# Dividing the mixer's input-projection tiles once and loading their parts from DRAM afterwards

## The chip, the cores and the metric

The kernel runs on one core of one Trainium2 chip. The metric is the device time of one execution in microseconds (us): the median of three runs before the change is 2557.08 us (2554.28 to 2558.01). About 0.2% (5 us) is what a measurement of this kernel can tell from no change.

## The reference

One decoder layer serves a prompt (2048 rows behind 16 prepended meta rows) and a sample group (8 sequences of 4 rows) with the same weights. All arithmetic is float32. Cut to what matters here:

```python
h = rmsnorm(x, norm_mix)
proj = h @ w_in                                  # 1024 -> 2560 + 8
lru_x, lru_gate, z, xbc, dt_raw = split(proj)    # 512, 512, 512, 1024, 8
xc  = causal_dwconv(lru_x, 4 taps);  hl = rg_lru(xc)          # a linear scan along the rows
lru_out = rmsnorm(hl * gelu(lru_gate), lru_out_norm)
xbc_c = silu(causal_dwconv(xbc, 4 taps));  ys = ssd_chunked(...)   # chunks of 128 rows, a state between them
ssd_out = rmsnorm(ys * silu(z), ssd_out_norm)
x = x + concatenate([lru_out, ssd_out]) @ w_out  # 1024 -> 1024
h = rmsnorm(x, norm_ffn)
u = causal_dwconv(h @ w_up, 3 taps);  x = x + (gelu(u[:, :3072]) * u[:, 3072:]) @ w_down
y = rmsnorm(x, norm_final)
```

The final states of the convolutions, of the LRU and of the SSD are outputs too.

## The kernel before, in words

**Divided operands.** TensorE multiplies in a rounded float32 format (F32R). To keep float32 accuracy each operand is divided into a high part (a rounded copy) and a low part (what the copy left): `divide` (L108) is one copy on ScalarE (`whi`, L109) and one subtraction on VectorE (`wlo`, L110). A product is then three matmuls, high by high, high by low, low by high. A weight tile is 128 x 1024 float32, 512 KB. The class `Plain` (L112) holds one: `load` brings it into a place with the tag `wraw` (two places), and `split` divides it into a pair of places with the tags `whi` and `wlo` (three pairs).

**Phase A, the mixer.** The rows are cut into six super-tiles (`PLAN_A`, L28): the sample and meta rows with two blocks of the prompt (N = 304 columns), then four of three blocks (N = 384), then one of two blocks (N = 256). For each super-tile all of `w_in` (20 weight tiles) and all of `w_out` (8 weight tiles) are loaded and divided again. The order of the main steps in one super-tile is: the small projection for dt; eight `xbc_main` steps; four `lru_main`; four `gate_main`; four `z_main`; then the output projection, `out_main` (L813): for each half of the output columns and each part of the inputs a pair of `w_out` tiles, and for each block of rows one step of 12 matmuls with 512 columns. A projection step (`project`, `group_mm`) takes one `w_in` tile and is 24 matmuls with N columns. The convolutions, gates, scans and chunks are side tasks, hung behind main steps by the table `SLOTS` (L41) and woven in by `weave` (L273).

**Phase B, the feed-forward part**, runs over four super-tiles of 512 rows; it has classes of its own for weights that it divides once and keeps in DRAM. The change does not touch them.

**What sets the order.** TensorE's order is as written. The order of the other engines, and that of the DMA issues on SyncE's queue (all DMAs of the kernel are issued there), is planned when the program is built, from estimated costs; a place with a tag is given on when all readers of the tile in it are done. The loop at the end of `build` (L297 to L316) walks the program: before each step it issues loads for weight tiles that are at most `AHEAD` = 2 past those the step uses, and divisions in the same way (none ahead until the first super-tile has begun, at `START2`).

**Rows of x.** `out_main` loads a 128 x 512 piece of x (`xo`, three places, L822), adds the product to it on VectorE (L826), and stores it to DRAM (`x2d`, L832) from SyncE's queue as soon as the second part is added. `Normed` (L161) normalises and transposes the rows of the next super-tile into `hhi` and `hlo`, both 128 x 8 x 546, in the pool `hh`, which stays open through phase A.

Of the kernel before, what the change touches and what calls it, by code (L numbers as in the profile page):

```python
# [8 lines left out]
F32 = mybir.dt.float32  # L9
F32R = mybir.dt.float32r  # L10
# [7 lines left out]
P = 128  # L18
D = 1024
NS, NSS, NM = 8, 4, 16  # L20
SROWS = NS * NSS
# [13 lines left out]
START = len(PLAN_A[0])  # L35
START2 = 3 * START + 1
GT_BUFS = 2
LOADS_B1, LOADS_B, SPLITS_B = 4, 3, 3


SLOTS = {  # L41
# [18 lines left out]
    "last": {  # L60
# [5 lines left out]
    },  # L66
# [7 lines left out]
def build(tc, i, o):  # L74
# [5 lines left out]
    with contextlib.ExitStack() as es:  # L80
# [5 lines left out]
        dp = es.enter_context(tc.tile_pool(name="scr", bufs=1, space=DRAM))  # L86
        xr = es.enter_context(tc.tile_pool(name="xr", bufs=1, side="right"))
        side = es.enter_context(contextlib.ExitStack())
        hh = side.enter_context(tc.tile_pool(name="hh", bufs=1, side="right"))
        phase = es.enter_context(contextlib.ExitStack())  # L90
        ja = phase.enter_context(tc.tile_pool(name="ja", bufs=1))
        junks = [lambda: ja.tile([P, D], BF16, name="junk", tag="junk")]
# [19 lines left out]
        class Plain:  # L112


            def __init__(self, src, room=lambda: wp.tile([P, 1024], F32, name="wraw", tag="wraw", bufs=2)):
                self.src, self.room = src, room
# [5 lines left out]
            def split(self, E=V):  # L122
                hi, lo = (wp.tile([P, 1024], F32R, name=nm, tag=nm) for nm in ("whi", "wlo"))
                divide(hi, lo, self.raw, E)
                self.out = hi, lo, self.raw

        def mms(ps, pairs):
            for k, (l, r) in enumerate(pairs):
# [32 lines left out]
        class Normed:  # L161


            def __init__(self, tiles):
                self.tiles = tiles
                self.h = None
                self.x = {}

            def alloc(self):
                if self.h is None:  # L170
                    self.h = [hh.tile([P, 8, NFMAX], F32R, name=nm, tag=nm) for nm in ("hhi", "hlo")]

            def load(self, q):
                src, off, rows = self.tiles[q]
# [109 lines left out]
                setattr(k, nm, v)  # L284

        k.tail = lambda: None
        h_b = Normed(b_tiles(k))
        phase_a(k, h_b)
        phase_b(k, h_b)

# [6 lines left out]
        for n, (fn, srcs) in enumerate(prog):  # L297
            if n < START:
                fn()
                continue  # L300
            if n == START2:
                begin.close()
            bound = len(flat) if n > k.begin_b else early
            b = n > k.begin_c
            while loaded < min(bound, used + len(srcs) + (LOADS_B if b else LOADS_B1 if n > k.begin_b else AHEAD)):
                flat[loaded].load()
                loaded += 1
            while split < min(bound, used + len(srcs) + (SPLITS_B if b else AHEAD if n >= START2 else 0)):
                flat[split].split(*(() if split else (G,)))
                split += 1  # L310
            ws = [z.out for z in flat[used:used + len(srcs)]]
            used += len(srcs)
            if fn is k.tail:
                end = es.enter_context(tc.manual_schedule(engines=order))
                continue
            fn(*ws)  # L316


def b_tiles(k):
    tiles, off = [], 0  # L320
    for t in PLAN_B[0]:
        rows = SROWS + 2 if t == "m" else P
        tiles.append((lambda t=t: (k.x2m if t == "m" else k.x2d[t], True), off, rows))
        off += rows
    return tiles
# [136 lines left out]
def phase_a_tile(k, E, c, si, columns, norm, norm2, x_src):  # L462
# [240 lines left out]
    def lru_main(j):  # L703
        def fn(w):
            T_.xc[j] = conv(j, project(w), c["lcw"][:, j, :], c["lcb"][:, j:j + 1], c["st_lc"][:, j], c["o_lc"][:, j])
        return fn
# [106 lines left out]
    def out_main(half, part, q):  # L813
        hcol = slice(half * 512, half * 512 + 512)

        def fn(*w):
            t, off, T = cols[q]
            if w:
                T_.w2 = w
            if part == 0:  # L820
                x = T_.xo[q] = tmp("xo", 512, bufs=3)
                ld(x[:T], x_src(t)[:, hcol])  # L822
            ps = psum("mm")
            k.tile_mm(ps, T_.w2, T_.y[0], T_.y[1], range(4 * part, 4 * part + 4), off, T)
            x = T_.xo[q]
            V.scalar_tensor_tensor(x[:T], ps[:T, :], T_.rs[part, q][:T], x[:T], op0=MUL, op1=ADD)  # L826
            if part == 1:
                if t == "m":
                    ld(k.x2m[0:SROWS, hcol], x[0:SROWS, :])
                    ld(k.x2m[SROWS:SROWS + 2, hcol], x[MISC - 2:MISC, :])  # L830
                else:
                    ld(k.x2d[t][:, hcol], x)  # L832
        return fn

    for j in range(8):
        main.append((xbc_main(j), (i["w_in"][12 + j],)))
    main.insert(int(first), (dt_main, ()))
    for j in range(4):
        main.append((lru_main(j), (i["w_in"][j],)))
    for j in range(4):  # L840
        main.append((gate_main(j), (i["w_in"][4 + j],)))
    for j in range(4):
        main.append((z_main(j), (i["w_in"][8 + j],)))
    for half in range(2):
        for part in range(2):
            for q in range(nt):
# [15 lines left out]
            tasks[f"misc{z}"] = lambda z=z: misc_blocks(3 * z, 3 * z + 3)  # L862

    if last:
        tasks["gain"] = lambda: ld(k.gain, i["gffn"])
    for q in range(nn):
        tasks[f"norm{q}"] = lambda q=q: norm2.norm(q)
# [525 lines left out]
```

## Time and profile before

| | us |
|---|---|
| median of three runs | 2557.08 |
| the profiled execution's own time | 2560.49 |
| its span, first to last instruction | 2558.4 |
| first super-tile of phase A, from 23 us | 160 |
| second to fifth super-tile, each | 158 to 160 |
| sixth super-tile | 121 |
| phase B, from 942 us | 1616 |

In the profile an engine's name stands for its work: PE matmul on TensorE, PEld its weight loads, DVE VectorE, ACT ScalarE, POOL GpSimd, SPq the queue of DMA issues on SyncE. A row of groups reads: line, engine, operation, out<-in by the program's names, shapes, count, then busy time, mean ns of one, idle time of the engine just before them, and what ended that idle time. A row of waits reads: who waited for whom, us in total, how often, the longest. A row of windows reads: stretch, length, busy us of each engine with its count of instructions, the granted TensorE clock, the busy share of the DMA engines, GB/s. Matmuls overlap: the duration of one is longer than the distance to the next.

### The profile page before, as it was taken

What the parts mean: (1) busy time and instruction counts of PE and PEld (TensorE: products, weight loads), DVE (VectorE), ACT (ScalarE), POOL (GpSimd) and SP (SyncE); (2) the same over time, 40 slices, a digit from 0 to 9 for tenths busy, and PEclk for the clock granted to TensorE, in tenths of its full rate; (3) what the DMA queues carried; (4) which work ended last, traced back from release to release, by engine and by line L of the source; (5) the groups of instructions that cost most, each with busy time, mean ns of one, the idle gap of its engine ahead of it and who ended that gap; (6) DMA issues with size and microseconds to landing.
All of it is one profiled execution on the core that took longest, in us unless ns stands there. A gap on an engine that the chain in (4) does not pass through costs nothing.

```text
span 2558.4 us, 42298 instructions
## 1 busy us (share of the span) xinstructions
PE 2450.5 (96%) x15834; PEld 2228.0 (87%) x15834; DVE 1953.8 (76%) x3028; ACT 1215.5 (48%) x2005; POOL 737.9 (29%) x1059
## 2 busy tenths in 40 slices
PE   7999998999999898999998999999999999999998
PEld 6788887888888888988886999998999998999997
DVE  7879878788787877776767877777877777877776
ACT  5545546455464655454455433434433434433333
POOL 5524333243242435545454201102101102100001
PEclk9999999999999999999999999999999999999999
DMA  5353252532525377554556866665866665866663
GB/s 183 119 180 98 90 173 70 183 98 87 171 75 173 110 229 257 185 198 178 197 201 236 300 249 226 221 218 214 313 227 214 214 220 189 316 214 214 218 223 123
DMA packets 153800, 486.39 MB, mean 190 GB/s; under 512 B 23334, under 2 KB 23718, under 8 KB 153596
## 3 DMA queue, kind: packets, MB, share of 16 engines
q1 hardware_dynamic: 153596, 483.70, 54.8%
q8 instruction: 125, 2.05, 0.3%
q14 instruction: 79, 0.65, 0.1%
HBM read 413.27 MB, written 70.37 MB: 189 GB/s over the span
## 4 chain that ended last, share of the span: by engine, by line
PE 60%; DVE 13%; issue 10%; POOL 7%; ACT 6%; DMA 4%; SPq 0%; POOLq 0%; DVEq 0%; ACTq 0%
PE mm L129 23%; PE sg L1116 14%; PE tr L129 9%; PE yy L129 9%; DVE cv L496 3%; DVE wlo L110 3%; ACT whi L109 2%; POOL wraw L958 2%; POOL wraw L957 1%; ACT ws L109 1%; POOL o_fc L1101 1%; POOL x L959 1%; DVE xi L741 1%; DMA wraw<-in_w_out 1%; DMA wk<-ws 1%
## 5 line engine op out<-in xcount | busy, mean ns | idle before, releaser
L110 DVE TENSOR_TENSOR wlo<-wraw,whi 128x1024 fp32r<-128x1024 f32 x358 | 456.0, 1275 | 147.3 <-ACT whi L109 146.3
L109 ACT ACTIVATE whi<-wraw 128x1024 fp32r<-128x1024 f32 x359 | 379.0, 1057 | 317.6 <-PE mm L129 141.8
L129 PE MATMUL mm<-hhi,whi 128*128 128x384 f32 (+4 forms) x1344 | 434.9, 324 | 13.9 <-ACT xr L491 10.5
L1116 PE MATMUL sg<-whi,ph 128*128 128x512 f32 x1320 | 425.1, 395 | 6.2 <-DVE acc L1120 6.2
L129 PE MATMUL mm<-hlo,whi 128*128 128x384 f32 (+4 forms) x1344 | 425.7, 317 | 0.9 <-DVE hlo L202 0.9
L129 PE MATMUL mm<-hhi,wlo 128*128 128x384 f32 (+4 forms) x1344 | 424.9, 316 | 0.0
L1101 POOL COPY o_fc<-u 128x2 f32<-128x2 f32 x192 | 85.9, 447 | 807.0 <-DVE u L1010 683.4
L1105 DVE SCALAR_TENSOR_TENSOR c<-u,fcw,c 128x512 f32<-128x512 f32 (+1 forms) x384 | 298.4, 791 | 23.0 <-ACT c L1103 13.4
L1116 PEld LDWEIGHTS sg<-whi,ph 128*128 128x128 f32 x1320 | 248.8, 189 | 65.5 <-DVE acc L1120 8.0
L129 PEld LDWEIGHTS mm<-hhi,whi 128*128 128x128 f32 x1344 | 258.3, 192 | 20.6 <-ACT xr L491 12.6
L129 PEld LDWEIGHTS mm<-hlo,whi 128*128 128x128 f32 x1344 | 257.8, 192 | 3.3 <-DVE hlo L202 1.2
L1116 PE MATMUL sg<-wlo,ph 128*128 128x512 f32 x660 | 259.7, 394 | 0.9 <-DVE wlo L110 0.9
L129 PEld LDWEIGHTS mm<-hhi,wlo 128*128 128x128 f32 x1344 | 257.9, 192 | 0.0
L1103 ACT ACTIVATE c<-u,fcb,fcw 128x512 f32<-128x512 f32 (+1 forms) x192 | 157.8, 823 | 111.8 <-DVE u L1010 109.2
L129 PE MATMUL yy<-h,ws 128*128 128x256 f32 x1476 | 195.5, 282 | 0.0
L129 PE MATMUL tr<-h,ws 128*128 128x256 f32 x1440 | 190.8, 282 | 1.2 <-DMA ws<-wk 1.2
L129 PE MATMUL mm<-h,ws 128*128 128x256 f32 x1404 | 185.9, 282 | 0.0
L129 PEld LDWEIGHTS yy<-h,ws 128*128 128x128 f32 x1476 | 184.8, 189 | 1.0
L129 PEld LDWEIGHTS tr<-h,ws 128*128 128x128 f32 x1440 | 180.1, 189 | 2.0 <-issue 1.3
L129 PEld LDWEIGHTS mm<-h,ws 128*128 128x128 f32 x1404 | 175.5, 189 | 0.5
L496 DVE SCALAR_TENSOR_TENSOR cv<-xr,packed,cv 128x384 f32<-128x384 f32 (+2 forms) x216 | 146.1, 677 | 6.9 <-ACT cv L494 4.2
L1120 DVE TENSOR_TENSOR acc<-acc,sg 128x512 f32<-128x512 f32 x165 | 112.7, 683 | 45.6 <-PE sg L1116 44.5
(311 smaller groups left out, 4983.7 us busy)
## 6 DMA issues: line engine op xcount, KB each, us to landing
ws<-wk SPq DMA_DIRECT2D x288, 512.0 KB, 5.0
wraw<-in_w_in SPq DMA_DIRECT2D x120, 512.0 KB, 3.6
wraw<-in_w_up SPq DMA_DIRECT2D x97, 512.0 KB, 4.7
wk<-ws SPq DMA_DIRECT2D x96, 512.0 KB, 6.6
wraw<-in_w_down SPq DMA_DIRECT2D x94, 512.0 KB, 4.9
wraw<-in_w_out SPq DMA_DIRECT2D x48, 512.0 KB, 3.6
wraw<-in_w_up SPq DMA_DIRECT2D x72, 256.0 KB, 5.5
x<-in_w_up SPq DMA_DIRECT2D x23, 512.0 KB, 6.8
```

Of the source, the lines that this page charges most:

```text
L109: A.activation(hi, raw, AF.Copy)
L110: E.tensor_tensor(lo, raw, hi.bitcast(F32), op=SUB)
L129: PE.matmul(ps, l, r, start=(k == 0), stop=(k == len(pairs) - 1))
L496: V.scalar_tensor_tensor(cv[:, 3:W], buf[:, t:t + NC], w[:, t:t + 1], cv[:, 3:W], op0=MUL, op1=ADD)
L741: V.tensor_tensor_scan(h[:, 3:W], a4[:, j, 3:W], m4[:, j, 3:W], hc[:, j:j + 1], op0=MUL, op1=ADD)
L957: G.tensor_tensor(v1, v0, v1, op=ADD)
L958: G.tensor_tensor(v0, g0, v0, op=SUB)
L1101: G.tensor_copy(o_fc[:, g, NS, :], u[:, W - 2:W])
L1103: A.activation(cv[:, 2:W], u[:, 2:W], AF.Identity, scale=fcw[:, g, 2:3], bias=c["fcb"][:, g:g + 1])
L1105: V.scalar_tensor_tensor(cv[:, 2:W], u[:, z:z + W - 2], fcw[:, g, z:z + 1], cv[:, 2:W], op0=MUL, op1=ADD)
L1116: PE.matmul(ps, l, r, start=first and n == 0, stop=last and n == len(seq) - 1)
L1120: V.tensor_tensor(xv, xv, ps, op=ADD)
```

## The change

In the first super-tile a `w_in` tile is loaded and divided as before, and both parts are also stored to DRAM, from ScalarE's queue: those of one tile are issued when the next one is divided. In the five later super-tiles a `w_in` tile is not divided: both parts are loaded from DRAM (two transfers of 512 KB in place of one), up to four tiles ahead. They go in turn into five places: three times the pair `whi` and `wlo`, then a new pair `xhi` and `xlo`, then the two `wraw` places. `w_out` tiles are loaded and divided as before, two ahead, through `wraw`. Loads of kept parts are not written before all divisions ahead of them are.

For room, `hhi` and `hlo` are 384 columns wide in phase A, in a pool `pa` beside the new pair, and in the last super-tile a new task `swap`, behind the last projection, closes that pool and opens `hh` with 546 columns for phase B's rows. The stores of `x2d` move from SyncE's queue to ScalarE's, each behind the addition of the next step.

```diff
-LOADS_B1, LOADS_B, SPLITS_B = 4, 3, 3
+LOADS_B1, LOADS_B, SPLITS_B, KEPT_AHEAD = 4, 3, 3, 4
...
-        15: "chunk41 norm0 lru1", 16: "norm1 lru2", 17: "norm2 lru3", 19: "ssd0 ssd1", 20: "rstd0 ssd2",
+        15: "chunk41 norm0 lru1", 16: "norm1 lru2", 17: "norm2 lru3", 19: "ssd0 ssd1", 20: "rstd0 ssd2 swap",
...
-        hh = side.enter_context(tc.tile_pool(name="hh", bufs=1, side="right"))
+        pa = side.enter_context(tc.tile_pool(name="pa", bufs=1, side="right"))
...
+        kept, late = {}, []
+
+        class Kept:
+
+            rooms = itertools.cycle("wwwxr")
+
+            def __init__(self, key, src):
+                self.key, self.plain = key, Plain(src)
+                self.ahead = KEPT_AHEAD
+
+            def load(self):
+                if self.key not in kept:
+                    kept[self.key] = [dp.tile([P, 1024], F32, name=f"{nm}_{self.key}", tag=f"{nm}_{self.key}")
+                                      for nm in ("khi", "klo")]
+                    self.plain.load()
+                    return
+                room = next(self.rooms)
+                if room == "w":
+                    parts = [wp.tile([P, 1024], F32R, name=nm, tag=nm) for nm in ("whi", "wlo")]
+                elif room == "x":
+                    parts = [pa.tile([P, 1024], F32R, name=nm, tag=nm) for nm in ("xhi", "xlo")]
+                else:
+                    parts = [wp.tile([P, 1024], F32, name="wraw", tag="wraw", bufs=2).bitcast(F32R) for z in range(2)]
+                for part, src in zip(parts, kept[self.key]):
+                    ld(part.bitcast(F32), src)
+                self.out = (*parts, None)
+
+            def split(self, E=V):
+                self.plain.split(E)
+                self.out = self.plain.out
+                store()
+                late.extend((z, part.bitcast(F32)) for z, part in zip(kept[self.key], self.out))
+
+        def store():
+
+            for dst, src in late:
+                A.dma_start(dst, src)
+            late.clear()
...
-                    self.h = [hh.tile([P, 8, NFMAX], F32R, name=nm, tag=nm) for nm in ("hhi", "hlo")]
+                    pool, n = (k.hh, NFMAX) if self.last else (pa, NMAX)
+                    self.h = [pool.tile([P, 8, n], F32R, name=nm, tag=nm) for nm in ("hhi", "hlo")]
...
-            while loaded < min(bound, used + len(srcs) + (LOADS_B if b else LOADS_B1 if n > k.begin_b else AHEAD)):
+            while loaded < bound:
+                ahead = LOADS_B if b else LOADS_B1 if n > k.begin_b else getattr(flat[loaded], "ahead", AHEAD)
+                if loaded >= used + len(srcs) + (ahead if n >= START2 else AHEAD):
+                    break
+                if getattr(flat[loaded], "key", None) in kept:
+
+                    if split < loaded:
+                        break
+                    split += 1
                 flat[loaded].load()
                 loaded += 1
-            while split < min(bound, used + len(srcs) + (SPLITS_B if b else AHEAD if n >= START2 else 0)):
+            while split < min(loaded, used + len(srcs) + (SPLITS_B if b else AHEAD if n >= START2 else 0)):
...
             V.scalar_tensor_tensor(x[:T], ps[:T, :], T_.rs[part, q][:T], x[:T], op0=MUL, op1=ADD)
+            k.store()
             if part == 1:
                 if t == "m":
-                    ld(k.x2m[0:SROWS, hcol], x[0:SROWS, :])
-                    ld(k.x2m[SROWS:SROWS + 2, hcol], x[MISC - 2:MISC, :])
+                    k.late.append((k.x2m[0:SROWS, hcol], x[0:SROWS, :]))
+                    k.late.append((k.x2m[SROWS:SROWS + 2, hcol], x[MISC - 2:MISC, :]))
                 else:
-                    ld(k.x2d[t][:, hcol], x)
+                    k.late.append((k.x2d[t][:, hcol], x))
+            if half == 1 and part == 1 and q == nt - 1:
+                k.store()
...
-        main.append((xbc_main(j), (i["w_in"][12 + j],)))
+        main.append((xbc_main(j), (k.Kept(12 + j, i["w_in"][12 + j]),)))
...
-        main.append((z_main(j), (i["w_in"][8 + j],)))
+        main.append((z_main(j), (k.Kept(8 + j, i["w_in"][8 + j]),)))
...
+        def swap():
+            k.side.close()
+            k.hh = k.side.enter_context(k.tc.tile_pool(name="hh", bufs=1, side="right", reuse_waits="tile"))
+        tasks["swap"] = swap
```

More of the change, by code (lines that the diff above doesn't have):

```diff
@@ L161, in build, with __init__ @@
         class Normed:
-            def __init__(self, tiles):
+            def __init__(self, tiles, last=False):
                 self.tiles = tiles
+                self.last = last
                 self.h = None
@@ L286, in build @@
         k.tail = lambda: None
-        h_b = Normed(b_tiles(k))
+        h_b = Normed(b_tiles(k), True)
         phase_a(k, h_b)
@@ L826, in fn @@
             V.scalar_tensor_tensor(x[:T], ps[:T, :], T_.rs[part, q][:T], x[:T], op0=MUL, op1=ADD)
+            k.store()
             if part == 1:
                 if t == "m":
-                    ld(k.x2m[0:SROWS, hcol], x[0:SROWS, :])
-                    ld(k.x2m[SROWS:SROWS + 2, hcol], x[MISC - 2:MISC, :])
-                else:
-                    ld(k.x2d[t][:, hcol], x)
+                    k.late.append((k.x2m[0:SROWS, hcol], x[0:SROWS, :]))
+                    k.late.append((k.x2m[SROWS:SROWS + 2, hcol], x[MISC - 2:MISC, :]))
+                else:
+                    k.late.append((k.x2d[t][:, hcol], x))
+            if half == 1 and part == 1 and q == nt - 1:
+                k.store()
         return fn
     for j in range(8):
-        main.append((xbc_main(j), (i["w_in"][12 + j],)))
+        main.append((xbc_main(j), (k.Kept(12 + j, i["w_in"][12 + j]),)))
     main.insert(int(first), (dt_main, ()))
     for j in range(4):
-        main.append((lru_main(j), (i["w_in"][j],)))
+        main.append((lru_main(j), (k.Kept(j, i["w_in"][j]),)))
     for j in range(4):
-        main.append((gate_main(j), (i["w_in"][4 + j],)))
+        main.append((gate_main(j), (k.Kept(4 + j, i["w_in"][4 + j]),)))
     for j in range(4):
-        main.append((z_main(j), (i["w_in"][8 + j],)))
+        main.append((z_main(j), (k.Kept(8 + j, i["w_in"][8 + j]),)))
     for half in range(2):
```

## The prediction

> **What bounds the kernel now.** I read the page first, then the windows by super-tile, then who waited for whom on TensorE in the five super-tiles that the change relieves, and then the chain of waits there.
>
> ```profile
> span 2558.4 us, 42298 instructions
> PE 2450.5 (96%) x15834; PEld 2228.0 (87%) x15834; DVE 1953.8 (76%) x3028; ACT 1215.5 (48%) x2005; POOL 737.9 (29%) x1059
> ```
>
> ```profile
> 23.00:183.00 160.00, 149.12 (x874) 123.16 (x873) 130.25 (x237) 83.89 (x173) 72.35 (x115) 0.96 0.44 142
> 183.00:341.00 158.00, 149.60 (x834) 133.98 (x833) 132.76 (x199) 86.42 (x140) 55.38 (x62) 1.00 0.39 124
> 821.00:942.00 121.00, 107.77 (x755) 97.96 (x754) 106.44 (x184) 73.70 (x137) 46.73 (x56) 0.97 0.54 158
> 942.00:2558.00 1616.00, 1580.16 (x10848) 1457.91 (x10846) 1175.87 (x1788) 703.70 (x1124) 388.25 (x621) 0.99 0.63 223
> ```
>
> TensorE is busy 96% of the span, and phase B (1616 us) is untouched: I take nothing from it. What the change can give lies between 183 and 942 us. There VectorE is busy for 132.76 of 158 us, so that it looks like a second bound, but only what TensorE waits for counts:
>
> ```profile
> PE yy L692 <- DVE yt L679: 14.9, 7, 2.6
> PE mm L129 <- ACT xr L491: 10.5, 8, 2.3
> PE sg L716 <- DVE cv L496: 8.0, 8, 2.3
> PE yy L666 <- DVE L L619: 4.4, 8, 1.4
> PE mm L129 <- ACT gq L769: 3.3, 2, 1.7
> PE tr L611 <- DVE xbc L592: 3.1, 1, 3.1
> PE mm L129 <- DVE wlo L110: 3.0, 4, 1.0
> PE mm L129 <- ACT whi L109: 0.5, 1, 0.5
> ```
>
> These are all waits but one of 0.5 us in that stretch, 47.7 us together. That is the size of the purse, however much work VectorE is spared.
>
> **Removed: 100 divisions.** Twenty in each of five super-tiles.
>
> ```profile
> L110 DVE TENSOR_TENSOR wlo<-wraw,whi 128x1024 fp32r<-128x1024 f32 x140 | 181.7, 1299 | 44.3 <-ACT whi L109 43.9
> L109 ACT ACTIVATE whi<-wraw 128x1024 fp32r<-128x1024 f32 x139 | 146.9, 1057 | 123.7 <-PE mm L129 92.0 <-DMA wraw<-in_w_out 20.9 <-DMA wraw<-in_w_in 9.7
> ```
>
> That is 100 x 1.299 = 130 us of VectorE and 100 x 1.057 = 106 us of ScalarE, and 40 of each, for `w_out`, stay. How much of it was in TensorE's way is told by what stands in the chain ahead of the waits, here of the second super-tile:
>
> ```profile
> 221.63 1.05 ACT whi L109
> 222.70 1.15 DVE wlo L110
> ...
> 244.89 4.23 PE mm L129 x24
> 249.16 1.76 DVE cv L496
> 250.92 0.61 DVE yt L679
> ...
> 268.33 2.63 DVE xi L741 x2
> 271.88 1.84 DVE xi L741 x2
> 274.17 0.60 DVE yt L679
> ```
>
> Ahead of the projection that waits for `xr` (at 223.1 us) stands a copy `whi` of 1.05 us on ScalarE: without it the wait of 1.1 us goes. But ahead of the two waits for `yt` stand a convolution tap and the scan, and no division: I leave their 14.9 us where they are. The 3.0 and 0.5 us for `wlo` and `whi` are `w_out`'s and stay as well. There remain 10.5 + 8.0 + 4.4 + 3.3 + 3.1 = 29.3 us, of which I take 25, since in some of these chains the division is shorter than the wait. A wait also costs clock:
>
> ```profile
> 53.71 0.70 PE L551 MATMUL yy<-dtm,packed 48*128 48x72 f32 x2 [3.32 <-DVE dtm L546]
> ```
>
> ```profile
> 54.00:60.00 6.00, 6.00 (x28) 5.87 (x28) 4.32 (x8) 0.82 (x4) 4.23 (x2) 0.60 0.29 90
> 60.00:63.00 3.00, 3.00 (x23) 3.00 (x22) 2.07 (x4) 2.88 (x13) 1.66 (x4) 1.00 0.00 0
> 126.00:131.00 5.00, 5.00 (x28) 5.00 (x28) 5.00 (x10) 1.94 (x4) 1.14 (x1) 0.66 0.33 105
> ```
>
> After TensorE had waited 3.32 us, it ran the next 6 us at 0.60 of its clock, 6 x 0.40 = 2.4 us lost; at 126 us it is 5 x 0.34 = 1.7 us. The clock is 0.97 in the sixth super-tile, so a few of the waits that go cost such a stretch too; I add 4 us. Gain: 29 us. Bounds: 15 (half of the 29.3), and 53 (all but `w_out`'s waits, 44.2, and five stretches of 1.7).
>
> **Moved: where the last projection's tile sits.** The five places go round as w, w, w, x, wraw, and 20 tiles are four rounds, so the twentieth tile, that of the last `z_main`, always sits in both `wraw` places. They come free only when its last matmul is done, and the first two `w_out` tiles need them. Today that is no matter: a `wraw` place is given on as soon as its tile is divided.
>
> ```profile
> SPq L120 <- DVE wlo L110: 855.0, 179, 17.0
> SPq L822 <- DMA x<-xo: 48.6, 20, 5.7
> ```
>
> ```profile
> L129 PE MATMUL mm<-whi,yhi 128*128 128x512 f32 x224 | 90.9, 406 | 0.6 <-ACT whi L109 0.5
> wraw<-in_w_out SPq DMA_DIRECT2D x40, 512.0 KB, 3.6
> ```
>
> The queue's loads of weights (L120) wait for `wlo`, not for TensorE, and the first matmul of an output group has waited 0.6 us in all of five super-tiles. After the change load, copy and subtraction all come between the last projection and the first output step, whose second matmul needs the low part: 3.6 + 1.06 + 1.30 = 6.0 us. TensorE's order is as written, and between the two steps in it stands at most the handful of tiny matmuls of `rstd0`; nothing hides it. The second `w_out` tile is loaded and divided behind the first, and is wanted six matmuls later. An idle time of 6.0 us is longer than the 3.32 us above, so I add 1.7 us of slow clock: 7.7 us, five times: 38 us. Bounds: 28 (5 x 5.7, no slow clock, the first matmul overlapped) and 5 x 10 = 50 (a landing of 5.4 us, as below, and 2.4 us of slow clock).
>
> The rows alone do not say that each idle time slows the clock: the second super-tile has two `yt` waits of up to 2.6 us at a clock of 1.00. The Trainium skill, page "TensorE: Matmul & The Clock Gate", section "Part 1: The HAM clock gate", states that the clock falls to half after an idle window of about 3.4 us and comes back after a busy one. By that rule the surcharge is there in all five, and the 38 us stand; without it the five could go without, and it would be 30 us. The trace agrees in that the slow stretches follow waits near 3 us.
>
> **Added: loads of both parts.** A projection of 384 columns takes 4.23 us in the chain, for 1.05 MB: 248 GB/s while projections follow each other closely.
>
> ```profile
> 22.00:35.00 13.00, 13.00 (x94) 12.10 (x94) 10.53 (x30) 8.48 (x17) 3.82 (x9) 1.00 0.79 274
> x<-in_x_p SPq DMA_DIRECT2D x8, 512.0 KB, 5.4
> ```
>
> 274 GB/s at a share of 0.79 puts the full rate near 347, so it fits, and four tiles ahead are 4 x 4.23 = 17 us for a landing of 3.6 to 5.4. At the start of a super-tile the second tile's place comes free only with the last output step, but the dt projection and the first projection then cover its landing. In the sixth super-tile a projection takes two thirds of 4.23 us, and 1.05 MB in 2.8 us is more than 347 GB/s; the five places in hand cover most of eight such steps. I take 0, with 0 to 3 us.
>
> **Added: stores in the first super-tile.** 40 x 0.524 = 21.0 MB. At 0.44 of the DMA engines for 142 GB/s the full rate is 323 GB/s there: 65 us of DMA time into 0.56 x 160 = 90 us that are free. It fits but for the start, where 0.79 is taken already: three tiles' stores, 3.1 MB or 9.7 us, meet 2.7 us of room in those 13 us, and the loads of weights share the engines. A place can also not be refilled before its store has landed.
>
> ```profile
> wk<-ws SPq DMA_DIRECT2D x96, 512.0 KB, 6.6
> 316.29 0.33 SPq L832 DMA_DIRECT2D x<-xo  x1
> ```
>
> A store of that size lands in 6.6 us in phase B, where four go together; three pairs of places at over 3 us a step bear that barely. Issuing costs about 40 x 0.33 = 13 us of ScalarE, which has 76 us free. I take 3 us, with 0 to 20. That the Trainium skill ("DMA: Bandwidth & Descriptors", "Issuing engines are not separate DMA queues") gives ScalarE's queue no engines of its own is why I count no relief from it; no run so far shows it.
>
> **Moved: `x2d` stores.** Behind the next step's addition and on ScalarE's queue, they land later, and the next half's `xo` loads wait for them (the 48.6 us above); SyncE's queue is in turn spared waiting for VectorE. VectorE can be late by some us there without TensorE seeing it, thanks to two product banks. I take 0, from -3 to +5. `swap` comes behind the last reader of what it closes: 0.
>
> **Sum.** On the profiled execution's own 2560.49 us (2.1 us beside its span): -29 + 38 + 3 = +12, 2572.5. The median of the three runs is 3.4 us lower: 2569.
>
> **Rivals.** *The waits come back whole* (faster): with VectorE at some 110 of 158 us the planner also moves `yt` forward, and the gain is 50 us, while the idle times stay at 30: 2557 - 50 + 30 + 3 = 2540. For it: the two `yt` waits recur in the same places, so one better order mends all. Against: no division stands in their chains. It decides where the gain passes 41 us. *No idle time before the output projection*, because the loads find a free place after all, so that this part doesn't do what it reads like: 2557 - 29 + 3 = 2531. Against it: two places with that tag, both in use. *They balance*: 38 gained, 36 lost, 3 for the stores: 2558. *The first super-tile chokes on its stores*, 20 us in place of 3: 2586.
>
> **How the numbers follow.** The forecast, 2569 us, has 0.52, with a range of its own from 2562 to 2586. Waits whole: 0.14. No idle time: 0.12. Balance: 0.15. Choked stores: 0.07. About 0.2%, 5 us, is what a measurement tells from no change. So faster has 0.14 + 0.12 = 0.26, same 0.15, slower 0.52 + 0.07 = 0.59. The range of 2538 to 2588 leaves out most of the case without idle time, a part of the waits returned whole, and the worst ends of the slow cases, some 0.2 in all.
>
> **What would show it.** Right: waits of TensorE at L129 for `whi` and `wlo` of five times about 5 to 6 us, with `wraw<-in_w_out` loads issued at the end of the last projection and a granted clock below 1 right after; `xr`, `cv`, `L`, `gq` and `xbc` waits down from 29 us to a few; `yt` unchanged; 100 fewer L109 and L110. Wrong: no wait at the head of the output projection, or super-tiles of 150 us or less, or a first super-tile much over 163 us.

## The result, and the profile after

| | before | after |
|---|---|---|
| median of five runs, us | 2557.08 (2554.28 to 2558.01) | 2571.78 (2569.27 to 2579.16) |
| the profiled execution's own time | 2560.49 | 2577.11 |
| ratio, 95% interval | | 1.0068 [1.0049, 1.0086] |

The changed kernel is 0.7% slower, 14.7 us by the medians. First its page: span and busy time of each engine.

```profile
span 2575.2 us, 42314 instructions
PE 2461.2 (96%) x15834; PEld 2233.6 (87%) x15834; DVE 1828.7 (71%) x2928; ACT 1123.5 (44%) x1905; POOL 665.8 (26%) x1059
```

VectorE lost 125 us of work and ScalarE 92, in 100 instructions each, and yet the span grew by 16.8 us. To see where, I cut phase A into super-tiles, each from its first dt matmul to that of the next (worked out from the start times in the trace). In these two kernels the first begins at 22.8 us. Each row is one profiled execution.

| us | first | 2nd | 3rd | 4th | 5th | 6th | phase B |
|---|---|---|---|---|---|---|---|
| before | 160.0 | 157.7 | 160.1 | 160.8 | 159.2 | 120.2 | 1617.7 |
| after | 185.8 | 157.6 | 157.6 | 157.0 | 155.8 | 117.6 | 1621.0 |

The first super-tile is 25.8 us longer, the five later ones only 12.4 us shorter together, and phase B 3.3 us longer, which is no more than it differs from run to run (1614.5 to 1621.6 us in this study). Now who waited for whom on TensorE in the five later ones, in the changed kernel (us in total, times, longest):

```profile
PE mm L168 <- ACT whi L109: 22.9, 5, 4.9
PE yy L741 <- DVE yt L728: 7.1, 4, 1.8
PE mm L168 <- DVE wlo L110: 3.2, 6, 0.7
PE tr L660 <- DMA xhi<-khi: 2.1, 1, 2.1
PE mm L168 <- DVE xo L875: 2.1, 2, 1.3
PE mm L168 <- ACT xr L540: 1.3, 1, 1.3
PE mm L168 <- DMA wlo<-klo: 1.1, 2, 0.6
...
PE yy L715 <- DVE L L668: 0.5, 3, 0.2
...
PE mm L168 <- ACT gq L818: 0.4, 1, 0.4
```

There are two stories in one view. `xr`, `gq`, `cv`, `L` and `xbc`, 29.3 us before, are down to 2.2 us together (no row is left of `cv` and `xbc`), and `yt` fell from 14.9 to 7.1, seven waits to four. At the top stands a new wait: five times, once in each super-tile, TensorE waits for `whi`, 4.6 us on average. The timeline of the changed kernel at the first of these places shows the chain (start, duration, engine and instruction; in brackets the idle time before it and what ended it):

```profile
320.64 0.34 PE L168 MATMUL mm<-hhi,wraw 128*128 128x384 f32 x1
320.83 8.28 SPq L120 DMA_DIRECT2D wraw<-in_w_out  x4
...
324.33 0.51 ACT L808 ACTIVATE gq<-ys 128x384 f32<-128x384 f32 x1
...
324.75 1.04 ACT L109 ACTIVATE whi<-wraw 128x1024 fp32r<-128x1024 f32 x1
...
325.82 1.24 DVE L110 TENSOR_TENSOR wlo<-wraw,whi 128x1024 fp32r<-128x1024 f32 x1 [0.74 <-ACT whi L109]
...
325.84 0.80 PE L168 MATMUL mm<-whi,yhi 128*128 128x512 f32 x1 [4.86 <-ACT whi L109]
...
327.12 0.79 PE L168 MATMUL mm<-wlo,yhi 128*128 128x512 f32 x1 [0.48 <-DVE wlo L110]
...
331.97 0.63 PE L168 MATMUL mm<-whi,yhi 128*128 128x512 f32 x1
...
332.40 0.44 PE L168 MATMUL mm<-wlo,yhi 128*128 128x512 f32 x1
...
332.68 0.39 PE L168 MATMUL mm<-whi,ylo 128*128 128x512 f32 x1
...
332.91 0.39 PE L168 MATMUL mm<-whi,yhi 128*128 128x512 f32 x1
```

The last matmul of the projection reads the `wraw` places and begins at 320.64; the loads into them are issued from 320.83 on, the copy begins at 324.75, the matmul at 325.84, and then the low part is late once more. (ScalarE was at work on `gq` just before the copy; whether the landing or ScalarE was last, these rows don't tell.) The rows also show the clock: matmuls follow each other every 0.43 us until 332.4, and every 0.23 us from 332.7 on. The windows of the changed kernel give the granted clock (column after the five engines) at the same place:

```profile
326.00:332.00 6.00, 5.52 (x13) 3.95 (x14) 2.29 (x2) 2.11 (x2) 0.00 (x0) 0.50 0.55 167
332.00:338.00 6.00, 6.00 (x28) 4.89 (x26) 2.95 (x4) 1.07 (x2) 0.00 (x0) 0.96 0.32 98
```

That is the rule of the Trainium skill on which the prediction drew ("TensorE: Matmul & The Clock Gate", "Part 1: The HAM clock gate": half the clock after an idle window of about 3.4 us), and this trace agrees: 0.50 for 6 us after a wait of 4.86.

The first super-tile's loss shows in the windows. Of the changed kernel:

```profile
22.00:35.00 13.00, 13.00 (x96) 12.07 (x95) 11.09 (x44) 5.93 (x14) 1.88 (x10) 1.00 1.02 392
35.00:50.00 15.00, 10.66 (x59) 10.42 (x58) 8.67 (x23) 6.32 (x12) 3.33 (x10) 0.77 1.00 380
...
85.00:105.00 20.00, 17.83 (x67) 11.02 (x66) 7.57 (x16) 6.33 (x12) 6.41 (x12) 0.74 0.70 229
```

And of the kernel before, the stretches that the prediction did not show:

```profile
35.00:50.00 15.00, 13.60 (x92) 12.99 (x91) 14.45 (x37) 11.91 (x27) 11.15 (x23) 0.95 0.36 113
...
85.00:105.00 20.00, 19.26 (x116) 14.10 (x116) 13.96 (x25) 6.12 (x13) 10.06 (x16) 1.00 0.55 178
```

Read the two columns before the last in each, TensorE's first. From 22 to 50 us the 16 DMA engines are full (1.02 and 1.00, 380 to 392 GB/s, where before it was 0.79 and 0.36). From 35 us on TensorE falls behind: 59 matmul records in place of 92, and later 67 for 116, at a clock of 0.77 and 0.74. The later stretches are no longer at the DMA engines' limit; work comes late there, and the waits cost clock besides. How a late landing reaches TensorE is seen once in the changed kernel, on ScalarE and then on TensorE:

```profile
38.77 1.06 ACT L109 ACTIVATE whi<-wraw 128x1024 fp32r<-128x1024 f32 x1 [4.03 <-DMA wraw<-in_w_in]
...
43.69 0.62 PE L168 MATMUL mm<-hhi,whi 128*128 128x304 f32 x1 [4.33 <-ACT xr L536]
```

ScalarE stands for 4.03 us until a tile of `w_in` has landed, then 2.40 us more for VectorE's `cv`, its next `xr` comes only at 43.2 us, and TensorE waits 4.33 us for that. Up to 145 us the median landing of a `w_in` tile is 5.4 us (3.6 before), and that of 512 KB of x rows 10.7 us (6.1 before).

### The profile page after: what moved, and what is told of

Its sections match the earlier page's. It is cut to its first block, busy times and chain, and to the rows that moved or that the text cites. A ratio compares the mean times of both kernels' runs of the same rounds, so it can differ in the third digit from the quotient of the medians.

```text
span 2575.2 us, 42314 instructions
## 1 busy us (share of the span) xinstructions
PE 2461.2 (96%) x15834; PEld 2233.6 (87%) x15834; DVE 1828.7 (71%) x2928; ACT 1123.5 (44%) x1905; POOL 665.8 (26%) x1059
## 4 chain that ended last, share of the span: by engine, by line
PE 66%; DVE 9%; issue 8%; POOL 7%; DMA 5%; ACT 5%; SPq 0%; POOLq 0%; ACTq 0%; DVEq 0%
PE mm L168 28%; PE sg L1172 14%; PE tr L168 9%; PE yy L168 9%; DVE wlo L110 2%; POOL wraw L1014 1%; ACT ws L109 1%; ACT whi L109 1%; POOL wraw L1013 1%; POOL o_fc L1157 1%; DVE cv L545 1%; POOL x L1015 1%; DMA wraw<-in_w_up 1%; DMA wk<-ws 1%; DVE xi L790 1%
## 5 line engine op out<-in xcount | busy, mean ns | idle before, releaser
L110 DVE TENSOR_TENSOR wlo<-wraw,whi 128x1024 fp32r<-128x1024 f32 x258 | 321.6, 1248 | 130.2 <-ACT whi L109 127.5
L109 ACT ACTIVATE whi<-wraw 128x1024 fp32r<-128x1024 f32 x259 | 272.9, 1056 | 243.2 <-PE sg L1172 90.1
L168 PE MATMUL mm<-hhi,whi 128*128 128x384 f32 (+4 forms) x1024 | 326.5, 319 | 7.7 <-ACT xr L536 6.5
L168 PE MATMUL mm<-hlo,whi 128*128 128x384 f32 (+4 forms) x1024 | 320.0, 312 | 0.9 <-DVE hlo L243 0.9
L168 PE MATMUL mm<-hhi,wlo 128*128 128x384 f32 (+4 forms) x1024 | 319.8, 312 | 1.1 <-DMA wlo<-klo 1.1
L168 PEld LDWEIGHTS mm<-hhi,whi 128*128 128x128 f32 x1024 | 197.7, 193 | 12.7 <-ACT xr L536 7.0
L168 PEld LDWEIGHTS mm<-hlo,whi 128*128 128x128 f32 x1024 | 197.3, 193 | 2.9 <-DVE hlo L243 1.2
L168 PEld LDWEIGHTS mm<-hhi,wlo 128*128 128x128 f32 x1024 | 197.1, 193 | 1.5 <-DMA wlo<-klo 1.5
L168 PEld LDWEIGHTS yy<-h,ws 128*128 128x128 f32 x1476 | 185.8, 189 | 1.0
L168 PE MATMUL mm<-h,ws 128*128 128x256 f32 x1404 | 185.8, 282 | 0.0
L1172 PEld LDWEIGHTS sg<-wlo,ph 128*128 128x128 f32 x660 | 124.1, 188 | 25.2 <-DVE wlo L110 1.1
```

What stands on the lines that cost most here:

```text
L109: A.activation(hi, raw, AF.Copy)
L110: E.tensor_tensor(lo, raw, hi.bitcast(F32), op=SUB)
L168: PE.matmul(ps, l, r, start=(k == 0), stop=(k == len(pairs) - 1))
L1172: PE.matmul(ps, l, r, start=first and n == 0, stop=last and n == len(seq) - 1)
```

## The experiments

My theory after the result: (1) the head of the output projection costs some 38 us, and only because of where the twentieth tile sits; (2) the stores cost some 20 us in the first super-tile; (3) what the divisions gave back is near 50 us, since the table has it: 12.4 + 38. The rivals: for (1) that something else ends there as soon as the wait goes; for (2) ScalarE's queue, SyncE's queue or the places that stores hold, in place of the DMA engines' rate; for (3) something else in the change, and not VectorE's work.

**The places turned round.** The twentieth tile then sits in the new pair, and both `wraw` places come free with the sixteenth tile, four projections earlier (the expectation says five).

```diff
-            rooms = itertools.cycle("wwwxr")
+            rooms = itertools.cycle("rwwwx")
```

> The five places go round as wraw, w, w, w, x instead of w, w, w, x, wraw, so that the twentieth tile of a super-tile sits in the new pair and the wraw places come free five projections earlier; nothing else is changed. Theory (the tile of the last projection in both wraw places keeps the output projection's first weights out): the five waits of TensorE for whi at the head of the output projection (22.9 us in the changed kernel) go, and with them the wait for the low part and the slow clock behind it, 6 to 7.7 us each: 30 to 38 us less, some 2534 to 2542 us. Rival (the wait only takes the place of work of VectorE and ScalarE that is late anyway, so that other waits grow in its stead): 10 us less or nothing, 2562 to 2572 us.

It took 2536.06 us, a ratio of 0.9905 [0.989, 0.992] to the kernel before. The waits of TensorE in its later super-tiles, 183 to 960 us:

```profile
PE yy L741 <- DVE yt L728: 7.0, 4, 1.7
...
PE mm L168 <- ACT xr L540: 2.8, 2, 1.4
...
PE mm L168 <- DVE wlo L110: 0.7, 2, 0.6
```

The wait for `whi` is gone and nothing of its size stands in its place. The five super-tiles take 149.4, 149.3, 149.7, 148.6 and 109.6 us, 39.0 us less than in the changed kernel. (1) is shown, by one letter's place in a string. Set against before, the same five are 51.4 us shorter: that is what the rest of the change gives there. (By the medians the turned places are worth 2571.78 - 2536.06 = 35.7 us; the changed kernel's profiled execution was 5 us above its median.)

**All tiles share one kept pair.** Only one tile's parts are stored, and all later loads read those; 38 of the 40 stores fall away.

```diff
-                    kept[self.key] = [dp.tile([P, 1024], F32, name=f"{nm}_{self.key}", tag=f"{nm}_{self.key}")
-                                      for nm in ("khi", "klo")]
+                    kept[self.key] = kept[12] if kept else [
+                        dp.tile([P, 1024], F32, name=nm, tag=nm) for nm in ("khi", "klo")]
...
-                late.extend((z, part.bitcast(F32)) for z, part in zip(kept[self.key], self.out))
+                if self.key == 12:
+                    late.extend((z, part.bitcast(F32)) for z, part in zip(kept[self.key], self.out))
```

> Left out: the parts of only one tile are stored in the first super-tile, and the five later super-tiles read that one tile's parts in all twenty places, with transfers of the same number and size. Theory (the first super-tile is 26 us longer than before because of its 40 stores): it falls back to about 160 us from the dt projection of the first to that of the second super-tile, some 26 us less, 2546 us. Rival (it is the planned order of the engines, which has changed there, and not the stores): the first super-tile stays some 20 us longer than before, 2565 us or more.

2551.74 us, 0.9968 [0.9954, 0.9983]. The first super-tile is back at 162 us, 24 less than with all stores (the whole time is 20.0 us less by the medians). So (2): the stores are what it costs, some 0.6 us for each of 38. In its windows the DMA engines have room again at 35 us, and TensorE keeps pace:

```profile
22.00:35.00 13.00, 13.00 (x93) 12.07 (x92) 11.62 (x37) 9.34 (x20) 5.81 (x14) 1.00 0.91 341
35.00:50.00 15.00, 13.07 (x96) 12.39 (x95) 14.01 (x39) 10.76 (x25) 8.94 (x19) 1.00 0.41 137
```

**Which resource the stores take.** Two candidates first. The planner had put one load of a kept part into the first super-tile, and SyncE's queue stood behind it, since it must wait for the store that it reads; here in the changed kernel, as a wait of that queue:

```profile
SPq L151 <- DMA khi<-whi: 4.9, 1, 4.9
```

One run puts the tile of the first super-tile's last projection into the new pair, so that no kept load finds room so early:

```diff
-                self.plain.split(E)
-                self.out = self.plain.out
+                if self.key == 11:
+                    hi, lo = (pa.tile([P, 1024], F32R, name=nm, tag=nm) for nm in ("xhi", "xlo"))
+                    divide(hi, lo, self.plain.raw, E)
+                    self.out = hi, lo, self.plain.raw
+                else:
+                    self.plain.split(E)
+                    self.out = self.plain.out
```

> The last projection's tile of the first super-tile is divided into the new pair xhi and xlo, which stood empty there, so that the load of a kept tile into that pair can't be issued in the middle of the first super-tile, where it holds SyncE's queue until the store that it reads has landed; the 40 stores stay. Theory A (SyncE's queue is held by that load at 38 us, and the loads of weights behind it are late): 8 to 14 us less, 2558 to 2564 us. Theory B (the DMA engines are full between 22 and 50 us whatever stands in the queue): at most 3 us less, 2569 us or more.

2575.8 us, 1.0054 [1.0033, 1.0075]: no gain, though its first super-tile is 5 us shorter in the profiled execution (as is that of the next run). The other run issues the stores (of parts and of `x2d`) from SyncE's queue:

```diff
-                A.dma_start(dst, src)
+                ld(dst, src)
```

> All stores of parts and of x2d are issued from SyncE's queue instead of ScalarE's, at the same places of the program. Theory (ScalarE's queue is not what makes the first super-tile long; bandwidth and SyncE's queue are): no gain, and 0 to 20 us more, since loads now wait behind stores that wait for VectorE: 2572 to 2592 us. Rival (the issues hold ScalarE, which waits in order for the low parts): the first super-tile gets back 10 us or more, 2562 us or less.

2573.32 us, 1.0047 [1.003, 1.0064]: no gain either. But the loss has moved, as this run's window and its longest wait of TensorE show:

```profile
35.00:50.00 15.00, 13.61 (x97) 12.68 (x97) 14.25 (x34) 9.10 (x23) 8.82 (x19) 1.00 0.88 292
...
PE yy L701 <- DMA sst<-in_st_ss: 12.8, 1, 12.8
```

From 35 to 50 us TensorE now keeps pace (13.61 of 15 us, 13.60 before) with the DMA engines at 0.88, and between 65 and 79 us it waits 12.8 us for one load. So the queue on which the stores are issued doesn't change what they cost in all, but it changes where and how; the equal times don't rule ScalarE's queue out for the changed kernel. The Trainium skill ("DMA: Bandwidth & Descriptors", "Issuing engines are not separate DMA queues") states that transfers issued from either queue run on the same 16 DMA engines. The nearly equal times, 2573.3 us from SyncE and 2571.8 from ScalarE, agree with that without proving it.

The first of these again, with the places turned round as well:

> On top of the kernel with the places in the order wraw, w, w, w, x (2536 us): the last projection's tile of the first super-tile is divided into the new pair, so that no kept tile is loaded into it in the middle of the first super-tile. Theory (what makes the first super-tile long is the DMA engines' rate, not SyncE's queue held at 38 us): within 5 us of 2536. Rival (the held queue): 8 us less or more than that, up to 2528 us.

2534.95 us, 0.9911 [0.9896, 0.9926], against 2536.06 without it: no difference in the time. Its first super-tile ends 3.0 us earlier (204.9 for 207.9 us).

**Work put back.** For (3), on top of the kernel with the places turned round, each load of a kept part is followed by a copy on ScalarE and a subtraction on VectorE of the same size as the division's, into a tile that nothing reads:

```diff
+                idle = pa.tile([P, 1024], BF16, name="idle", tag="idle")
+                A.activation(idle, parts[0].bitcast(F32), AF.Copy)
+                V.tensor_tensor(idle, parts[0].bitcast(F32), idle, op=SUB)
```

> On top of the kernel with the places in the order wraw, w, w, w, x (2536 us): for each of the 100 kept tiles one copy of its high part on ScalarE and one subtraction on VectorE, 128 x 1024 each, into a tile that nothing reads, are put back; loads, places and stores stay. Theory (the gain of 51 us in the five later super-tiles is the work that VectorE and ScalarE no longer do): super-tiles of 149 us go back to 157 to 161, 40 to 55 us more, 2576 to 2591 us. Rival (the gain comes from weights that lie ready four ahead, not from the engines): 10 us more or less, 2536 to 2546 us. In the prediction's accounting, by which only waits with a division in their chain came back: 29 us more, 2565 us.

2577.6 us, 1.008 [1.006, 1.010]: 41.5 us over 2536. Then with the subtraction alone:

```diff
+                idle = pa.tile([P, 1024], BF16, name="idle", tag="idle")
+                V.tensor_tensor(idle, parts[0].bitcast(F32), parts[1].bitcast(F32), op=SUB)
```

> As the run before, but only the subtraction on VectorE is put back, 100 times 1.25 us, and no copy on ScalarE. Theory (VectorE is what TensorE waits for in these super-tiles, directly or through ScalarE): three quarters or more of the 40 to 55 us come back, 2566 us or more. Rival (ScalarE's copies, which stood ahead of the evacuations xr, are the larger part): 20 us or less, up to 2556 us.

2583.72 us, 1.0093 [1.0071, 1.0115]: 47.7 us over. The later super-tiles are 159.1, 158.5, 159.1, 154.8 and 123.5 us, 48.4 more than without it. (That less work put back costs more than both, 2583.7 for 2577.6 us, stays unexplained; the two intervals overlap.) TensorE's longest waits in them:

```profile
PE yy L588 <- DVE dtA L571: 11.3, 4, 4.1
PE mm L170 <- ACT xr L542: 8.6, 4, 4.2
PE yy L743 <- DVE yt L730: 8.1, 4, 2.0
PE sg L767 <- DVE cv L547: 4.9, 4, 1.6
```

`xr` and `cv` are back; `yt` has hardly moved from the 7.0 us without the subtraction, and the largest, for `dtA`, is one that the kernel before did not have. But VectorE also stood still in this run, for the landings of what it subtracts (`idle`) and, ahead of the divisions of `w_out`, for their copies:

```profile
DVE wlo L110 <- ACT whi L109: 20.6, 14, 2.1
DVE idle L154 <- DMA wlo<-klo: 16.4, 8, 3.4
...
DVE idle L154 <- DMA wraw<-klo: 6.1, 6, 2.0
```

With 1.1 us for `whi` that is 23.6 us for landings, and up to 24 us of the 48 could be these. The divisions of before did not run without standing still either: the row of L110 in the prediction has 44.3 us of idle time ahead of them, and here it is 20.6 + 23.6 = 44.2. So this run is close to the kernel before in both, but does not tell the one from the other. The last two runs use an operand that always stands in SBUF, `gain`, once for VectorE and once for ScalarE:

```diff
+                V.tensor_tensor(idle, gain, gain, op=SUB)
```

> Like the kernel with the places turned round, but at each of the 100 loads of kept parts VectorE also subtracts a 128x1024 constant from itself, about 1.22 us each and 122 us in all, into a tile that nothing reads; no other part is changed or left out. Unlike the run that subtracted the loaded parts (2583.7 us), its operand always stands in SBUF, so that VectorE never stands still for a landing (there it did for 23.6 us in all). Theory W, VectorE's time itself was what the divisions cost: most of the 47.7 us comes back again, 30 to 48 us over 2536, so 2566 to 2584 us. Theory D, VectorE standing still for landings made most of that number: 5 to 20 us over, 2541 to 2556 us, and then the 51 us that the five super-tiles gained can't all be VectorE's work.

```diff
+                A.activation(idle, gain, AF.Copy)
```

> The same with ScalarE in VectorE's place: at each of the 100 loads of kept parts it copies a 128x1024 constant, about 1.06 us each and 106 us in all, into a tile that nothing reads; no other part is changed or left out. Theory W, VectorE alone was in the way: within 8 us of 2536, so at most 2544 us. Rival, the copies ahead of xr, cv and gq in ScalarE's order cost as well: 12 to 25 us over, 2548 to 2561 us.

2583.97 us, 1.0098 [1.0082, 1.0115], and 2538.99 us, 0.9924 [0.9907, 0.9941]. By the medians that is theory W twice, but the trace shows that the work did not stand where I had meant it: with nothing to wait for, the planner drew it forward. Of the 100 subtractions 46 run in the first super-tile, 52 in the second, and 2 later; of the copies 77 run in the second. The windows of the run with the subtractions, for the second and the third super-tile:

```profile
224.00:400.00 176.00, 155.65 (x829) 137.68 (x827) 167.08 (x230) 68.03 (x119) 74.79 (x62) 0.95 0.49 169
400.00:549.00 149.00, 146.98 (x829) 133.04 (x828) 108.58 (x178) 67.57 (x119) 44.48 (x62) 1.00 0.57 201
```

And of the run with the copies, the second:

```profile
206.00:362.00 156.00, 150.68 (x830) 134.96 (x829) 108.41 (x178) 139.69 (x196) 45.42 (x62) 0.98 0.55 192
```

Each run thus holds its own comparison: the third super-tile, with none of it, is 149 us in both. In the second, 52 subtractions cost 176.4 - 149.4 = 27.0 us, 0.52 us each, with no landing to wait for; 77 copies cost 156.3 - 149.4 = 6.9 us, 0.09 each. Before, 20 divisions in each super-tile stood for 51.4 / 100 = 0.51 us each.

That 0.52 and 0.51 agree says less than it seems. VectorE's 108.6 us of other work and 52 times 1.22 us are 172 us, more than the 149 us that the super-tile takes without them: there VectorE itself is the bound, busy for 167 of 176 us, while before it was busy for 133 of 158. ScalarE's 67.6 us and 77 times 1.06 us would also fill 149 us, and cost only 6.9. What is shown, then: taking work from VectorE is what gave most of the gain, and ScalarE's copies by themselves give little (the runs with 100 subtractions spread as before bring 41 to 48 of the 51 us back). The price of one subtraction at 20 in a super-tile, with nothing to wait for, was not measured: if all 23.6 us for landings came on top, 24.8 of the 48.4 us are left for the work itself.

**Where the stores stand.** In this and the next runs the places are turned round. The parts of the eight `xbc` tiles, 16 of the 40 stores, are stored in the second super-tile in place of the first; these tiles are divided in both.

```diff
-        main.append((xbc_main(j), (k.Kept(12 + j, i["w_in"][12 + j]),)))
+        main.append((xbc_main(j), (k.Kept(12 + j, i["w_in"][12 + j], si == 1),)))
...
-                late.extend((z, part.bitcast(F32)) for z, part in zip(kept[self.key], self.out))
+                if self.keep:
+                    late.extend((z, part.bitcast(F32)) for z, part in zip(kept[self.key], self.out))
```

> On top of the kernel with the places in the order wraw, w, w, w, x (2536 us): the parts of the eight xbc tiles are stored in the second super-tile and not in the first, so that these eight are divided once more; the other twelve as before. Theory (the first super-tile's 26 us come from the start, where loads and 16 of the stores together ask more than the DMA engines give between 22 and 50 us, and what is late there stays late): the first super-tile loses 15 to 24 us, the second grows by 4 to 10 (eight divisions, and stores beside its loads), in all 5 to 20 us less, 2516 to 2531 us. Rival (any 40 stores cost about 0.6 us each wherever they stand): the first gives back 10 us and the second takes 10 or more, no gain, 2536 us or more.

2534.81 us, 0.9907 [0.9891, 0.9924]. The first super-tile is 11.2 us shorter, less than the theory's 15 to 24, and the second 9.9 longer (159.3 for 149.4). Nothing is won, as the rival had it. But part of the second's 9.9 us is the eight divisions that stand there again (an estimate of 4 us at 0.51 each), so that 16 stores cost some 6 us there and 11 in the first.

**The places that stores hold.** A place can't be refilled before its store has landed. One run gives the first super-tile a fourth pair of places; the other stores one tile's parts 20 times over, from a pair that holds still, so that no store holds a place that is wanted.

```diff
+            pairs = itertools.cycle([(wp, "whi", "wlo")] * 3 + [(pa, "xhi", "xlo")])
...
-                self.plain.split(E)
-                self.out = self.plain.out
+                pool, a, b = next(self.pairs)
+                hi, lo = (pool.tile([P, 1024], F32R, name=nm, tag=nm) for nm in (a, b))
+                divide(hi, lo, self.plain.raw, E)
+                self.out = hi, lo, self.plain.raw
```

> On top of the kernel with the places in the order wraw, w, w, w, x (2536 us): in the first super-tile every fourth tile is divided into the new pair xhi and xlo, so that divided tiles have four pairs of places there instead of three; the 40 stores stay. Theory P (a pair can't be refilled before its store has landed, and three pairs don't bear that): the first super-tile, 185 us from the first to the second dt projection, goes back to 160 to 172 us, 13 to 25 us less, 2511 to 2523 us. Theory B (the DMA engines' rate at the start is the limit, whatever the places): 5 us or less, 2531 us or more.

```diff
-                self.plain.split(E)
-                self.out = self.plain.out
+                if self.key == 12:
+                    hi, lo = (pa.tile([P, 1024], F32R, name=nm, tag=nm) for nm in ("xhi", "xlo"))
+                    divide(hi, lo, self.plain.raw, E)
+                    kept["still"] = self.out = hi, lo, self.plain.raw
+                else:
+                    self.plain.split(E)
+                    self.out = self.plain.out
...
-                late.extend((z, part.bitcast(F32)) for z, part in zip(kept[self.key], self.out))
+                late.extend((z, part.bitcast(F32)) for z, part in zip(kept[self.key], kept["still"]))
```

> Left out: all 40 stores are made from the parts of the first tile, which stay in the pair xhi and xlo for the whole first super-tile, so that later super-tiles read that one tile's parts; number, size, queue and places in the program of the stores are those of the kernel with the places in the order wraw, w, w, w, x, but no store holds a whi or wlo place. Theory P (places held by stores): the first super-tile goes back from 185 to 160 to 166 us, 2511 to 2517 us. Theory B (rate of the DMA engines): it stays at 178 us or more, 2529 us or more.

With four pairs it is 2529.53 us, 0.9887 [0.987, 0.9905], the best of the study and 1.1% less than before; the first super-tile is 9.7 us shorter (198.2 - 207.9). With the still pair it is 2532.06 us, 0.990 [0.9871, 0.9928], and 4.7 us shorter; the 4 us between this and 2536.06 are within the two intervals. The first number lies between what the two theories had expected, the second near the one by the DMA rate. Windows of the kernel with four pairs, then of the one with the still pair:

```profile
35.00:50.00 15.00, 10.22 (x58) 9.98 (x57) 9.14 (x25) 6.47 (x13) 3.71 (x12) 0.77 0.91 347
```

```profile
35.00:50.00 15.00, 10.06 (x58) 9.82 (x57) 9.03 (x26) 6.33 (x15) 3.91 (x14) 0.77 0.91 347
```

In both the DMA engines are full from 22 to 35 us (1.03 and 1.00), and from 35 to 50 TensorE is as far behind as in the changed kernel, 10 of 15 us busy. Both also take the new pair in the first super-tile, which alone was worth 3.0 us there, so held places are some 2 to 10 us of the 26; the other 16 to 24 go with the stores' traffic. How much of those is the engines' rate by itself, and how much the order of work planned around the stores, stays open. The run with the stores on SyncE's queue, where TensorE kept pace from 35 to 50 us and lost 12.8 us later behind one load, suggests that the order has a part in it.

## Why the prediction came out

The time, 2569 us, came within 3 us of the measured 2571.78, and the sign was right. The sum was +12 us on the profiled execution, and it grew by 16.6. Of the three terms that make it, one was right and two were wrong by nearly the same amount in opposite directions.

| term, us | predicted (bounds) | measured |
|---|---|---|
| divisions removed | -29 (-53 to -15) | -51.4 |
| head of the output projection | +38 (28 to 50) | +39.0 |
| stores in the first super-tile | +3 (0 to 20) | +25.8 |
| phase B | 0 | +3.3 |

These measured terms add up to +16.7. Each is a difference between single profiled executions; by the medians the head is worth 35.7 us, and 38 of the 40 stores 20.0.

**The head of the output projection** was right in place, mechanism and size. Load, copy and subtraction, predicted at 6.0 us, show as 4.86 + 0.48 = 5.3 us at the first of the five; the slow clock, predicted at 1.7 us, is 3.0 us by the window there (6 us at 0.50). Together that is 8.3 us, and the second super-tile grew shorter by 157.6 - 149.4 = 8.2 when the places were turned round. The run with the places turned round undoes it alone.

**The gain** was mis-sized: 51 us for 29. The step that failed is "ahead of the two waits for `yt` stand a convolution tap and the scan, and no division: I leave their 14.9 us where they are". They fell to 7.1 us. The step is half right: of the two waits in a super-tile, the one behind the scan stands as it was, 1.8 us in each of four super-tiles. The other, 2.6 us behind the convolution tap in each of three, is gone. VectorE's order at that place, before and then in the changed kernel:

```profile
246.51 2.24 DVE L724 SCALAR_TENSOR_TENSOR m<-th 128x384 f32<-128x384 f32 x1 [0.72 <-POOL th L723]
248.67 2.25 DVE L496 SCALAR_TENSOR_TENSOR cv<-xr,packed,cv 128x384 f32<-128x384 f32 x1
250.84 0.68 DVE L679 TENSOR_TENSOR yt<-yy,ex 128x512 f32<-128x512 f32 x1
```

```profile
266.12 0.68 DVE L728 TENSOR_TENSOR yt<-yy,ex 128x512 f32<-128x512 f32 x1
266.92 1.38 DVE L773 SCALAR_TENSOR_TENSOR m<-th 128x384 f32<-128x384 f32 x1
```

`yt` now stands ahead of `m`: the planner has moved it forward, as the prediction's first rival said. Reading the pieces ahead of a wait was right for the wait behind the scan; for the other it took the order of those pieces as given, and the order changed. What in the plan moved it is not shown: with the subtractions put back, `yt` still waits only four times, 8.1 us in all.

The second error is to take the sum of TensorE's waits for the purse. With the places turned round, on which the 51.4 us were measured, all of TensorE's waits in these super-tiles went from 48.2 to 13.8 us, by 34.4. About 10 us more came as clock, for which the prediction had taken 4: the granted clock was 0.97 to 1.00 in these super-tiles before, and is 1.00 now. The other 7 us are in pieces that no row of waits names, and stay open. The bound of 53 did hold it. The rival that the waits come back whole described this half well (50 us), and lost because the stores were not 3 us.

**The stores** were mis-sized: 26 us for 3, beyond the bound of 20. The step that failed is "It fits but for the start", priced at 3 us. The average of 0.44 over 160 us hid that the first stores, 14 of the 40 up to 50 us, meet the stretch that was nearest to full. There they fill the DMA engines for 28 us, the weights and the rows of x land later, and TensorE is still behind 50 us on, with a slow clock on top; how much of this is the rate and how much the order stays open, as said. The rival of choked stores had the mechanism, at 20 us; nothing weighed it together with a whole gain.

**The loads of both parts**, taken at 0, were right: TensorE waited 3.2 us in all for kept parts between 183 and 960 us (`xhi` 2.1 and `wlo` 1.1). The moved `x2d` stores were right at 0 as far as the waits tell: TensorE waits 2.1 us for `xo`, all at the end of the first super-tile, and the wait of SyncE's queue for these stores, 48.6 us before, is in the changed kernel

```profile
SPq L871 <- DMA x<-xo: 44.6, 19, 6.6
```

What would have shown it wrong was named ahead: "a first super-tile much over 163 us" came true (185.8), "`yt` unchanged" did not. That the forecast held was luck: two errors, 22 and 23 us, cancelled.

## What to carry to other kernels

When tiles go round through places that another stage also needs, look at where the last one of the round sits: here one letter moved in a string of five was worth 36 us, more than twice the loss of the whole change. Price a burst of transfers in the stretch where it falls, with that stretch's own share of the DMA engines, and not by an average over the stage. And when much work goes from an engine whose order is planned, expect the plan to change with it: neither the piece ahead of a wait nor the sum of the waits holds all that can be gained.

## What the runs showed of the hardware

Moving loads and stores together, the DMA engines of this core reached 380 to 392 GB/s at a share of 1.00 to 1.02, more than the 347 that the prediction had worked out from loads alone; the stores still did not fit. (The row with one tile stored, 341 GB/s at 0.91, would give 375 in the prediction's way, so busy share and rate are not strictly proportional.) An idle time of 4.86 us on TensorE was followed by 6 us at a granted clock of 0.50, with matmuls of 512 columns every 0.43 us in place of 0.23. And 77 copies of 1.06 us more on ScalarE in one super-tile cost 6.9 us with the engine busy for 140 of 156 us, while 52 subtractions of 1.22 us on VectorE, busy for 167 of 176, cost 27: more work than fits into the stage.
